# First weights behind two input tiles, own tiles for the third and fourth job's weights, and a measuring stream ahead of the split

## The chip, the cores and the metric

The kernel runs on one core of one Trainium2 chip, in one launch. The metric is the device time of an execution in microseconds (us). Engine names: TensorE is PE (its weight loads are PEld), VectorE is DVE, ScalarE is ACT, GpSimd is POOL, and SyncE is SP, whose queue issues the transfers.

## The reference

One layer of a streaming encoder trunk over 2048 prompt frames and 32 sample frames, D = 1024. What matters here is its start:

```python
hp = layer_norm(x_prompt, ln0_g, ln0_b)
qa, ka, va, za, qkv_b, zb, a_b, b_b, gate_a, gate_b = split_projection(x @ w_in)
```

The input is normalised and multiplied by `w_in`, of 1024 x 6160. Of the products, `gate_a` and `gate_b` (2 x 1024 columns) are needed only at the end; `a_b` and `b_b` (16 columns) give the decays of a gated delta rule (branch B), `qkv_b` its queries, keys and values through a causal convolution; the rest feeds chunk-band attention (branch A). Both branches are projected, gated, merged, projected again and normalised.

## The kernel before

Precision comes from splitting: each float32 operand becomes a half-precision high part and a half-precision rest, and a product is three passes on TensorE (high by high, high by weights' rest, input's rest by high). Weights are first scaled by a power of two that comes from their own sum of squares.

The prompt is done in two halves of 1024 columns. `build_h` loads eight input tiles of 128 frames (512 KB each), takes mean and variance on VectorE, normalises there, transposes on TensorE, adds gain and bias on ScalarE (`q` = 0) or VectorE (`q` = 1) into `tmp`, casts to the high part `hi` on ScalarE and subtracts the rest `lo` on GpSimd. Tiles 4 to 7 take their statistics only after the mark `first`: the last `tmp` of tile 3 is written (line 534). The marks `h_ready` and `l_ready` say when a tile's parts are there.

A job is one tile of 128 weight columns (1024 x 128, in two transfers of 256 KB). `all_jobs` gives their order: in the first half two gate jobs, then `ab` (the 16 decay columns; its rest shares the tile `whi` with its high part, and it has two blocks of 512 columns), then the convolution's jobs. Three coroutines serve them:

- `fetch` loads `wraw` (two buffers, `raw_gate`),
- `divide` waits for a `whi`/`wlo` pair (two buffers, `w_gate`), and, in the first half, squares the weights on ScalarE with an accumulated sum `w_sq`; `power` sums over the partitions with a small matmul and makes the scale on VectorE, GpSimd (a power) and VectorE again; then ScalarE scales and casts and GpSimd subtracts, in two pieces of 512,
- `multiply` runs the passes, block by block; with the last block of a job it gives `w_gate` back. The first two jobs run together, in blocks of 256, 256 and 512 columns (`FIRST[0]`), each block for both jobs in turn. Results go to two banks (`pj`); a job's `evac` reads them and frees the bank.

The order of the instructions on each engine is fixed when the program is built, by a planner (`Flow`): every coroutine has a clock, each operation is priced, and the one with the earliest clock goes on. On the chip each engine runs its list in this order and waits for real semaphores. The planner prices a transfer on SyncE's queue so:

```python
start = max(self.cur.clock + 0.2, self.busy.get(queue, 0.0)) + 0.5
end = max(start + 0.6, self.busy.get("DMA", 0.0)) + size / 200e3
return end + MARGIN        # 1.6
```

where rows of under 768 bytes count as 768. `yield` with a number moves a coroutine's clock to that time. `flow.start(x, 2.0)` starts one at clock 2.0.

When `l_ready[0][7]` is set (the last `lo` of the first half), the main thread goes on: `phase_b` clears 17 block-diagonal tiles of 128 x 1024 on VectorE in one go (`k_bd`, `qk_bd`, `q_bd`, `kd_bd`, `u_bd`), and then opens the phase; only then can the `ab` job's `evac` run, which needs a tile of that phase (`open_job` waits for it). The phase's queue of blocks follows: decays, convolution, the delta rule's systems, its recurrence.

The profile puts nearly all instructions on line 260, a helper; so groups are told by their tiles: `whi` written from `wraw` with 128x1024 elements is the square, with 128x512 the cast; `wlo` the split; `b<-w_sq` the sum's matmul; `pj` the products; `sig` the gate jobs' evac; `ab` that of the decay columns.

Of the kernel before, what the change touches and what calls it, by code (L numbers as in the profile page):

```python
# [13 lines left out]
F16 = mybir.dt.float16  # L14
# [7 lines left out]
P = 128  # L22
D = 1024
KD = D // P
# [244 lines left out]
def trunk(ctx: ExitStack, tc: tile.TileContext, x_p, x_s, cache_k, cache_v, st_conv, st_gdn,  # L269
# [197 lines left out]
    def build_h(half, xpool, nx):  # L467

        hT[half] = [None, None]
        ncols = HCOLS[half]  # L470
        nt = 4 - half
        x_gate, t_gate = gate(nx), gate(nt)
        freed, first = [mark(), mark()], mark()
        sizes = [SPLIT, ncols - SPLIT]
        tiles = [(n + P - 1) // P for n in sizes]

        def free(b):
            yield h_free[b]
            w = SPLIT if b == 0 else HALF + DEC - SPLIT
            hT[half][b] = [hpool.tile([P, KD, w], F16, tag=f"{x}{b}", name=f"{x}{half}{b}") for x in ("hi", "lo")]  # L480
            freed[b].done()

        def one(b, t, rows):
            c0 = t * P
            gt = half * 8 + b * 4 + t
            xt = xpool.tile([P, D], F32, tag="x", bufs=nx, name=f"x{gt}")
            yield dma(xt[:rows], x_s if rows < P else x_p[gt * P:(gt + 1) * P, :])
            if half == 0 and b == 1:
                yield first
            st = xpool.tile([P, 2, 6], F32, tag="st", bufs=nx, name=f"st{gt}")  # L490
            for i in range(2):
                V.bn_stats(out=st[:rows, i, :], in_=xt[:rows, i * 512:(i + 1) * 512])
                yield
            V.bn_aggr(out=mv[:rows, gt, :], in_=st[:rows])
            V.tensor_scalar(out=mv[:rows, gt, 1:2], in0=mv[:rows, gt, 1:2], scalar1=LN_EPS,
                            scalar2=None, op0=ALU.add)
            yield
            rsqrt(mv[:rows, gt, 1:2], mv[:rows, gt, 1:2])
            yield
            V.tensor_scalar(out=xt[:rows], in0=xt[:rows], scalar1=mv[:rows, gt, 0:1],  # L500
                            scalar2=mv[:rows, gt, 1:2], op0=ALU.subtract, op1=ALU.mult)
            yield freed[b]
            hi, lo = hT[half][b]
            todo = [2, 2, 2]

            def part(q):
                tag = "ba"[q] if half == 0 else "b"
                yield t_gate
                yield scaled
                yield bank[tag]  # L510
                tp = pt(tag)
                for k in range(4):
                    kk = 4 * q + k
                    PE.transpose(tp[:, k * P:k * P + rows], xt[:rows, kk * P:(kk + 1) * P],
                                 ident[:rows, :rows])
                todo[0] -= 1
                if not todo[0]:
                    x_gate.give()
                yield
                tmp = xpool.tile([P, 4, P], F32, tag="tmp", bufs=nt, name=f"tmp{gt}{q}")  # L520
                m = tmp[:, :, 0:rows]
                ks = slice(4 * q, 4 * q + 4)
                for k in range(4):
                    kk = 4 * q + k
                    src, g, b_ = tp[:, k * P:k * P + rows], ln0gT[:, kk:kk + 1], ln0bT[:, kk:kk + 1]
                    if q == 0:
                        S.activation(out=tmp[:, k, 0:rows], in_=src, func=AF.Identity, scale=g, bias=b_)
                    else:
                        V.tensor_scalar(out=tmp[:, k, 0:rows], in0=src, scalar1=g, scalar2=b_,
                                        op0=ALU.mult, op1=ALU.add)  # L530
                    if k == 1:
                        yield
                bank[tag].give()
                if b == 0 and t == 3 and q == 1:
                    first.done()
                yield
                hv_ = hi[:, ks, c0:c0 + rows]
                S.copy(out=hv_, in_=m)
                todo[1] -= 1
                if not todo[1]:  # L540
                    h_ready[half][gt - half * 8].done()
                yield
                (V if q == 0 and half == 1 else G).tensor_tensor(out=lo[:, ks, c0:c0 + rows], in0=m,
                                                                 in1=hv_, op=ALU.subtract)
                t_gate.give()
                yield
                todo[2] -= 1
                if not todo[2]:
                    l_ready[half][gt - half * 8].done()

            for q in range(2):
                flow.start(part(q))

        for b in range(2):
            flow.start(free(b))
        for b in range(2):
            if half == 0 and b == 1:

                yield 3.0
            for t in range(tiles[b]):  # L560
                yield x_gate
                flow.start(one(b, t, min(P, sizes[b] - t * P)))

# [7 lines left out]
    class Job:  # L571
# [3 lines left out]
        def __init__(self, half, wid, src, evac=None, key=None, cols=P, blocks=None):  # L575
            self.wid = wid
            self.half, self.src, self.evac, self.cols, self.key = half, src, evac, cols, key
            self.end = self.two = False
            self.blocks = blocks or BLOCKS[half]

    NRAW = 2
    raw_gate, w_gate, sig_slots = gate(NRAW), gate(2), gate(2)
    q_raw, q_w = Queue(flow), Queue(flow)

    def fetch(jobs):

# [33 lines left out]
        V.tensor_scalar(out=inv, in0=half_, scalar1=h_scale[:, 2:3], scalar2=None, op0=ALU.mult)  # L620
        V.tensor_scalar(out=half_, in0=half_, scalar1=h_scale[:, 3:4], scalar2=None, op0=ALU.mult)

    def divide():

        while True:
            job, raw, t = yield from q_raw.get()
            yield w_gate
            hi = wpool.tile([P, KD, P], F16, tag="whi", bufs=2, name="whi")
            lo = wpool.tile([P, KD, P], F16, tag="wlo", bufs=2, name="wlo")
            sc = w_scale[:, job.wid:job.wid + 1]  # L630
            yield t
            if job.half == 0:
                S.activation(out=hi[:], in_=raw[:], func=AF.Square, accum_out=w_sq[:])
                yield
                yield from power(sc, w_sq[:])
                flow.start(factors(job.wid))
            src, main = raw[:, :, 0:job.cols], hi[:, :, 0:job.cols]
            S.activation(out=src, in_=src, func=AF.Copy, scale=sc)
            for i in range(2):
                ks = slice(4 * i, 4 * i + 4)  # L640
                S.copy(out=main[:, ks], in_=src[:, ks])
                yield

                rest_ = lo[:, ks] if job.cols == P else hi[:, ks, job.cols:P]
                G.tensor_tensor(out=rest_, in0=src[:, ks], in1=main[:, ks], op=ALU.subtract)
                if i:
                    raw_gate.give()
                    q_w.put((job, hi, lo))
                yield
# [14 lines left out]
    def multiply():  # L664

        while True:
            some, todo = [], [(0, 0)]
            while todo:
                bi, which = todo.pop(0)
                if which == len(some):  # L670
                    some.append((yield from q_w.get()))
                    job = some[which][0]
                    if which == 0:

                        todo = [(b, w) for b in range(len(job.blocks)) for w in range(1 + job.two)][1:]
                    if job.key:
                        job.open = mark()
                        flow.start(open_job(job))
# [16 lines left out]
                for k in range(KD):  # L695
                    PE.matmul(ps[:, 0:n], wh[:, k], hl[:, k, :], start=False, stop=(k == KD - 1))
                    if k == KD - 1:
                        last = bi == len(job.blocks) - 1
                        if job.end and (bi == 0 or last):
                            h_free[0 if bi == 0 else 1].give()  # L700
                        if last:
                            w_gate.give()
                    yield
                flow.start(evac(job, bi, c0, n, gcol, ps))
# [1234 lines left out]
    def marked():  # L1939

        ahead, half = [], None
        for job in all_jobs():
            if job.half != half:
# [3 lines left out]
                ahead, half, n = [], job.half, 0  # L1947
                job.two = True
            n += 1
            if n <= 2:  # L1950
                if job.key is None:
                    job.blocks = FIRST[half]
# [262 lines left out]
            all_done.done()  # L2215


    with ExitStack() as stack0:
        open_banks(stack0, "ps0", a=3)
        xp = stack0.enter_context(tc.tile_pool(name="x0", bufs=1, reuse_waits="tile"))  # L2220
        flow.start(norm_params(xp))
        flow.start(build_h(0, xp, 8))
        flow.start(fetch(marked()), 2.0)
        flow.start(setup(xp), 20.0)
        flow.start(setup2(xp), 30.0)
        flow.start(spread(), 100.0)
        flow.start(divide())
        flow.start(multiply())
        flow.run(l_ready[0][7])
    for half in range(2):  # L2230
        stack, make, done = phase_b(half)
        enter(1, half, make)
        flow.run(done)
        stack.close()
        if half:
            wr_pool.append(ctx.enter_context(tc.tile_pool(name="wr0", bufs=1)))
            wr_open.done()
# [70 lines left out]
```

## Time and profile before

| | before |
|---|---|
| median of 3 runs | 2084.61 us (2081.7 to 2089.64) |
| profiled execution, its own time | 2083.65 us |
| its span | 2081.6 us |
| TensorE busy | 1968.6 us (95%) |
| VectorE busy | 1499.7 us (72%) |
| ScalarE busy | 978.1 us (47%) |
| GpSimd busy | 633.1 us (30%) |
| moved by DMA | 196.49 MB, mean 94 GB/s |

The share of busy time is a mean over stages. TensorE is busy nearly all the time, so time can be found only where it idles; a row of the timeline gives the start in us, the duration, the engine, what is written from what, and, in brackets, the idle time before it and what ended that.

### The profile page before, as it was taken

How to read it: one execution, taken by the hardware profiler on the slowest of the kernel's cores; microseconds unless marked ns; L12 is line 12 of the kernel's file. 1: busy time of each engine (PE TensorE's matmuls, PEld its weight loads, DVE VectorE, ACT ScalarE, POOL GpSimd, SP SyncE). 2: the span in 40 equal slices, each digit the busy share in tenths (PEclk: the TensorE clock that was granted, in tenths of full speed). 3: DMA queues.
4: the chain of work that ended last, by engine and by line, in shares of the span. 5: the costliest groups of instructions: out<-in, count | busy, mean ns of one | idle time of the engine just before them, and what ended most of it. 6: DMA issues, size and time to landing. Idle time of an engine off the chain costs nothing. (4 is left out here: it accounts for less than half of the span.)

```text
span 2081.6 us, 41386 instructions
## 1 busy us (share of the span) xinstructions
PE 1968.6 (95%) x15098; PEld 1411.3 (68%) x15098; DVE 1499.7 (72%) x4661; ACT 978.1 (47%) x2098; POOL 633.1 (30%) x708
## 2 busy tenths in 40 slices
PE   4999999999999999998999999999999988999998
PEld 3454666766465657566667777667666777888996
DVE  7679889873377758679998986356656667666775
ACT  5565554444466667564544543355656641111110
POOL 6244333422312113243332331311011134433342
PEclk9999999999999999999999999999999999999999
DMA  3233232323423233122233233332232445433331
GB/s 119 72 92 106 75 102 57 100 80 91 116 86 111 70 92 100 65 85 72 66 89 83 77 99 84 105 92 76 72 88 88 129 137 175 132 102 122 102 116 54
DMA packets 197719, 196.49 MB, mean 94 GB/s; under 512 B 79622, under 2 KB 147570, under 8 KB 197516
## 3 DMA queue, kind: packets, MB, share of 16 engines
q1 hardware_dynamic: 197516, 193.85, 31.6%
q8 instruction: 119, 1.95, 0.4%
q14 instruction: 84, 0.69, 0.1%
HBM read 135.91 MB, written 50.53 MB: 90 GB/s over the span
## 5 line engine op out<-in xcount | busy, mean ns | idle before, releaser
L260 PE MATMUL pj<-hi,whi 128*128 128x512 f16 (+2 forms) x1992 | 644.8, 339 | 10.4 <-DVE zb L260 2.7
L260 PE MATMUL pj<-hi,wlo 128*128 128x512 f16 (+2 forms) x1952 | 635.9, 338 | 2.4 <-POOL wlo L260 2.3
L260 PEld LDWEIGHTS <-whi 128*128 128x128 f16 x3984 | 413.5, 105 | 214.5 <-issue 3.9
L260 PE MATMUL pj<-lo,whi 128*128 128x512 f16 (+2 forms) x1992 | 457.7, 340 | 0.0
L260 POOL TENSOR_TENSOR wlo<-wraw,whi 128x512 f16<-128x512 f32 x192 | 226.9, 1184 | 585.9 <-ACT whi L260 313.0
L260 PEld LDWEIGHTS <-wlo 128*128 128x128 f16 x1952 | 204.8, 105 | 111.1 <-issue 10.7
L260 ACT CAST mh<-sg 128x256 fp32r<-128x256 f32 x64 | 25.9, 406 | 279.6 <-DVE sg L260 279.6
L260 ACT CAST ph<-b 128x512 f16<-128x512 f32 (+2 forms) x224 | 93.1, 421 | 100.0 <-PE b L260 96.8
L260 DVE TENSOR_TENSOR pl<-b,ph 128x512 f16<-128x512 f32 (+2 forms) x224 | 107.7, 485 | 44.7 <-ACT ph L260 43.1
L260 PE MATMUL a<-ghi,whi 128*128 128x256 f32 (+1 forms) x512 | 132.6, 290 | 6.3 <-DVE sg L260 6.2
L260 DVE TENSOR_TENSOR sys_u<-sys_u,sys_t 128x60 f32<-128x60 f32 (+23 forms) x527 | 129.3, 251 | 6.7
L260 ACT ACTIVATE wraw<-wraw,w_scale 128x1024 f32<-128x1024 f32 (+1 forms) x98 | 111.5, 1138 | 46.6 <-DVE w_scale L260 42.9
L260 PE MATMUL a<-ghi,wlo 128*128 128x256 f32 (+1 forms) x512 | 130.3, 285 | 0.0
L260 ACT CAST whi<-wraw 128x512 f16<-128x512 f32 (+1 forms) x196 | 119.4, 612 | 20.9 <-PE pj L260 18.0
L260 DVE TENSOR_TENSOR sys_t<-sys_u,sys_p 128x60 f32<-128x60 f32 (+21 forms) x459 | 121.2, 265 | 6.1
L260 ACT ACTIVATE sb<-sb,mx,unit 128x640 f32<-128x640 f32 (+4 forms) x128 | 108.8, 851 | 20.0 <-DVE mx L260 19.7
L260 DVE SCALAR_TENSOR_TENSOR acc<-raw,cwT,acc 128x512 f32<-128x512 f32 x144 | 114.0, 792 | 5.4 <-ACT acc L260 4.4
L260 POOL TENSOR_TENSOR w_scale<-w_scale,mhalf 128x1 f32<-128x1 f32 x49 | 30.9, 631 | 269.3 <-DVE w_scale L260 204.2
L260 PE MATMUL b<-ident,sb 128*128 128x128 f32 x560 | 100.6, 279 | 5.3 <-ACT sb L260 2.2
L260 PEld LDWEIGHTS a<-ghi,whi 128*128 128x128 f32 x512 | 98.0, 191 | 9.0 <-DVE sg L260 7.8
L260 ACT COPY v_t<-o 128x64 f32<-128x64 f32 x132 | 27.7, 210 | 161.1 <-PE o L260 133.3
L260 PEld LDWEIGHTS a<-ghi,wlo 128*128 128x128 f32 x512 | 97.8, 191 | 0.3
(350 smaller groups left out, 4221.8 us busy)
## 6 DMA issues: line engine op xcount, KB each, us to landing
wraw<-in_w_in SPq DMA_DIRECT2D x192, 256.0 KB
sg<-sig SPq DMA_DIRECT2D x112, 128.0 KB
sig<-sig SPq DMA_DIRECT2D x44, 256.0 KB
sys_p<-sol_p SPq DMA_DIRECT2D x17, 512.0 KB
x<-in_x_p SPq DMA_DIRECT2D x16, 512.0 KB
xt<-in_x_p SPq DMA_DIRECT2D x16, 512.0 KB
out_y_p<-xt SPq DMA_DIRECT2D x16, 512.0 KB
glo<-g SPq DMA_DIRECT2D x14, 512.0 KB
```

The lines of the kernel that those rows point to most:

```text
L260: r = f(*a, **k)
```

## The change

- `fetch` starts at the planner's clock 1.0 instead of 2.0, and `build_h` issues the first half's tiles 2 and 3 only at 2.0. So the transfers of the first two jobs' weights stand behind input tiles 0 and 1, ahead of 2 and 3; tiles 4 to 7 follow as before.
- The third job (`ab`) and the fourth get tiles of their own from a new pool `first_w` (6 KB per partition), which is opened ahead of the first stage's pool and closed after branch B's first half. They neither wait for `w_gate` nor give it.
- `divide` is cut in two: `measure` takes a job from `fetch`, waits for its tiles and its data, squares and makes the scale; `divide` takes it from there by a queue `q_scaled`. Behind a square the planner's clock is moved on by 0.4.
- The first two jobs' run takes in the third: the order of (block, job) is (0,0), (1,0), (0,1), (1,1), (0,2), (2,0), (2,1), (1,2), where it was (0,0), (0,1), (1,0), (1,1), (2,0), (2,1).

```diff
@@ build_h
             for t in range(tiles[b]):
+                if half == 0 and b == 0 and t == 2:
+                    yield 2.0
                 yield x_gate
                 flow.start(one(b, t, min(P, sizes[b] - t * P)))
...
-    q_raw, q_w = Queue(flow), Queue(flow)
+    q_raw, q_scaled, q_w = Queue(flow), Queue(flow), Queue(flow)
...
-    def divide():
+    def measure():
 
         while True:
             job, raw, t = yield from q_raw.get()
-            yield w_gate
-            hi = wpool.tile([P, KD, P], F16, tag="whi", bufs=2, name="whi")
-            lo = wpool.tile([P, KD, P], F16, tag="wlo", bufs=2, name="wlo")
+            if job.own:
+                hi, lo = job.own
+            else:
+                yield w_gate
+                hi = wpool.tile([P, KD, P], F16, tag="whi", bufs=2, name="whi")
+                lo = wpool.tile([P, KD, P], F16, tag="wlo", bufs=2, name="wlo")
             sc = w_scale[:, job.wid:job.wid + 1]
             yield t
             if job.half == 0:
                 S.activation(out=hi[:], in_=raw[:], func=AF.Square, accum_out=w_sq[:])
-                yield
+                yield flow.cur.clock + 0.4
                 yield from power(sc, w_sq[:])
                 flow.start(factors(job.wid))
+            q_scaled.put((job, raw, hi, lo))
+            yield
+
+    def divide():
+
+        while True:
+            job, raw, hi, lo = yield from q_scaled.get()
+            sc = w_scale[:, job.wid:job.wid + 1]
             src, main = raw[:, :, 0:job.cols], hi[:, :, 0:job.cols]
...
                         todo = [(b, w) for b in range(len(job.blocks)) for w in range(1 + job.two)][1:]
+                        if job.blocks is FIRST[0]:
+
+                            todo = [(1, 0), (0, 1), (1, 1), (0, 2), (2, 0), (2, 1), (1, 2)]
...
-                        if last:
+                        if last and not job.own:
                             w_gate.give()
...
             n += 1
+            if half == 0 and 2 < n <= 4:
+                job.own = [first_w.tile([P, KD, P], F16, name=f"{x}{n}") if x == "whi" or job.cols == P else None
+                           for x in ("whi", "wlo")]
+            if half == 0 and n == 3:
+                yield job
+                continue
...
+    stack_w = ExitStack()
+    first_w = stack_w.enter_context(tc.tile_pool(name="first_w", bufs=1, reuse_waits="tile"))
...
-        flow.start(fetch(marked()), 2.0)
+        flow.start(fetch(marked()), 1.0)
...
+        flow.start(measure())
         flow.start(divide())
...
         stack.close()
+        stack_w.close()
```

More of the change, by code (lines that the diff above doesn't have):

```diff
@@ L578, in __init__ @@
             self.end = self.two = False
+            self.own = None
             self.blocks = blocks or BLOCKS[half]
```

## The prediction

> **What bounds the kernel now.** I read the page first: its head, then the line of TensorE in part 1 and in the 40 slices.
>
> ```profile
> span 2081.6 us, 41386 instructions
> ...
> PE 1968.6 (95%) x15098; PEld 1411.3 (68%) x15098; DVE 1499.7 (72%) x4661; ACT 978.1 (47%) x2098; POOL 633.1 (30%) x708
> ...
> PE   4999999999999999998999999999999988999998
> ```
>
> TensorE is busy 1968.6 of 2081.6 us and has a 4 in one slice alone, the first. So the kernel is bound by TensorE, and a change of the start can win only what TensorE idles there. The busy times by stretch (columns: stretch, its length, each engine's busy time, granted clock) say how much that is.
>
> ```profile
> 0.00:20.00 20.00, 5.59 (x23) 4.68 (x24) 14.56 (x51) 7.71 (x15) 7.83 (x15) 1.00 0.73 272
> 20.00:40.00 20.00, 11.42 (x67) 9.23 (x65) 17.81 (x50) 13.72 (x31) 15.05 (x16) 1.00 0.08 10
> 40.00:60.00 20.00, 15.56 (x95) 11.14 (x96) 15.42 (x27) 9.31 (x20) 9.41 (x8) 0.83 0.15 48
> 60.00:80.00 20.00, 16.67 (x80) 7.51 (x79) 9.76 (x20) 10.74 (x18) 6.60 (x9) 1.00 0.23 76
> 80.00:100.00 20.00, 19.90 (x148) 9.77 (x146) 13.81 (x33) 17.43 (x25) 5.68 (x10) 1.00 0.18 64
> ```
>
> Of the first 80 us TensorE idles 80 - 5.59 - 11.42 - 15.56 - 16.67 = 30.8 us; from 80 us on it is full (19.90 of 20). From 0 to 40 VectorE is the busy one (17.81 of 20 in the second stretch): it normalises eight input tiles. Now the timeline of TensorE, at the places where the blocks of the first jobs begin.
>
> ```profile
> 31.64 0.42 PE L260 MATMUL pj<-hi,whi 128*128 128x256 f16 x1
> ...
> 48.35 0.33 PE L260 MATMUL pj<-hi,wlo 128*128 128x256 f16 x1 [1.94 <-POOL wlo L260]
> ...
> 49.75 1.92 PE L260 MATMUL pj<-lo,whi 128*128 128x256 f16 x8
> ...
> 53.41 1.04 PE L260 MATMUL pj<-lo,whi 128*128 128x256 f16 x8
> ...
> 56.91 0.38 PE L260 MATMUL pj<-hi,whi 128*128 128x512 f16 x1
> ...
> 62.09 0.38 PE L260 MATMUL pj<-hi,whi 128*128 128x512 f16 x1
> ...
> 70.45 1.47 PE L260 MATMUL pj<-hi,whi 128*128 128x512 f16 x6 [2.67 <-POOL whi L260]
> ...
> 74.06 1.89 PE L260 MATMUL pj<-hi,whi 128*128 128x512 f16 x8
> ...
> 77.51 0.38 PE L260 MATMUL pj<-hi,whi 128*128 128x512 f16 x1
> ...
> 79.62 0.38 PE L260 MATMUL b<-w_sq,tiny 128*128 128x1 f32 x2 [0.65 <-ACT whi L260]
> ```
>
> The first weights serve from 31.64, the second only from 48.35 (1.94 us of wait for their low half), the blocks of the second half of the columns run at 56.91 and 62.09, the third job (the 16 decay columns) waits 2.67 us for its weights and takes 70.45 to 77.51, and the fourth job begins at 77.51. That last time is my yardstick: whatever stands behind it is a full TensorE.
>
> Why the weights are late is in the timelines of ScalarE, GpSimd and VectorE.
>
> ```profile
> 17.66 1.05 ACT L260 ACTIVATE whi<-wraw 128x1024 f16<-128x1024 f32 x1
> 24.48 1.15 ACT L260 ACTIVATE wraw<-wraw,w_scale 128x1024 f32<-128x1024 f32 x1 [0.45 <-DVE w_scale L260]
> 25.66 0.62 ACT L260 CAST whi<-wraw 128x512 f16<-128x512 f32 x1
> 34.34 1.05 ACT L260 ACTIVATE whi<-wraw 128x1024 f16<-128x1024 f32 x1
> 62.29 1.06 ACT L260 ACTIVATE whi<-wraw 128x1024 f16<-128x1024 f32 x1 [4.66 <-PE pj L260]
> 67.87 0.69 ACT L260 ACTIVATE sig<-pj,w_half 128x512 f32<-128x512 f32 x1 [3.85 <-issue]
> ```
>
> ```profile
> 42.69 1.16 POOL L260 TENSOR_TENSOR wlo<-wraw,whi 128x512 f16<-128x512 f32 x1
> ...
> 48.26 2.27 POOL L260 TENSOR_TENSOR lo<-tmp,hi 128x512 f16<-128x512 f32 x2
> ```
>
> ```profile
> 24.56 0.68 DVE L260 BATCH_NORM_STATS2 st<-x 128x6 f32<-128x512 f32 x1
> ...
> 44.99 1.37 DVE L260 TENSOR_SCALAR tmp<-a,ln0gT,ln0bT 128x128 f32<-128x128 f32 x4 [2.44 <-POOL lo L260]
> 46.52 0.91 DVE L260 MEMSET k_bd<- 128x1024 f32 x1 [0.16 <-issue]
> ...
> 63.71 0.91 DVE L260 MEMSET u_bd<- 128x1024 f32 x1 [0.16 <-issue]
> ...
> 65.30 0.15 DVE L260 TENSOR_SCALAR w_scale<-w_scale 128x1 int32<-128x1 int32 x1 [0.67 <-POOL w_scale L260]
> 75.68 0.74 DVE L260 SCALAR_TENSOR_TENSOR ab<-pj,w_inv,ab 40x512 f32<-40x512 f32 x1 [1.94 <-ACT ab L260]
> ```
>
> The squares that measure jobs 1, 2 and 3 stand at 17.66, 34.34 and 62.29; the third had to wait until TensorE was through with the first weights (their tile is reused). The last low half of the input ends at 48.26 + 2.27 = 50.53. And right behind the last tile VectorE clears 17 block-diagonal tiles, 46.52 to 64.62 (63.71 + 0.91), in one piece: nothing that stands behind them in its order runs earlier.
>
> **The change part by part.**
>
> Order of the loads. Two rows of SyncE's queue, the second the third job's raw weights:
>
> ```profile
> 3.33 2.03 SPq L283 DMA_DIRECT2D wraw<-in_w_in  x4
> ...
> 35.99 2.03 SPq L283 DMA_DIRECT2D wraw<-in_w_ab  x4
> ```
>
> Four issues of 0.5 us go ahead of input tiles 2 and 3, and their 1 MB is about 3.9 us at the 272 GB/s of the first 20 us: tiles 2 and 3 land up to 4 us later. VectorE covers it with tiles 0 and 1 while it has work on them; without that cover it is the loss that stands below. The planner prices an input tile at 2.62 us, a weight tile at 2 x 1.97 (its 512-byte rows count as 768), one after another, plus 1.6. In its clock the first two weight tiles come at 13.7 and 17.6 instead of 18.9 and 22.9, input tiles 2 and 3 at 20.2 and 22.9 instead of 12.4 and 15.0, and tiles 4 to 7 as before. This clock sets only the order of the instructions. By it the first square moves among the work on tile 0, and the first split ends, by my own pass through the order, near 25 instead of 34; the second near 31 instead of 48. On the chip I take the same shifts. TensorE then has the first four 256-column blocks (2.6 us each, half of the 62.09 - 56.91 = 5.2 of a 512-column block; 10.4 in all) done among the transposes before tile 7 is ready. These blocks stop counting.
>
> Tiles 4 to 7 wait for the last of tile 3 (mark "first"). In the order their statistics move back from 25.5 to about 30.9. Real cost: VectorE loses the head start that it had on tiles 2 and 3 (two tiles, four statistics of 0.68 = 2.7 us), and ScalarE and GpSimd get back what the second job's scale, two casts and two splits took among tiles 4 to 7: 1.15 + 2 x 0.62 and 2 x 1.16, 2.4 us each. I take 49.5 for the last low half, 1 us earlier than the 50.53 of now; ends 47.5 (the 2.4 are won, nothing lost) and 53 (the 2.7 lost, nothing won).
>
> Third job. Its own tile takes away the wait at 62.29, and block 0 of it stands before the second half of the columns. In the order its raw weights land at 43.6 and its scale is through VectorE at about 47.5 to 48; the 17 clears are issued when tile 7 is done, at about 51.5 by the same pass. So the scale stands before the clears, by some 4 us of planner clock. Its split ends at about the same time as tile 7, so TensorE idles some us ahead of it.
>
> The sum, from 49.5 on, on TensorE alone. Start of the third job's block 0 at +0.5 (hand-over); the block 74.06 - 70.45 = 3.6, and 1.7 more for a slow start (below); block 2 of job 1: 62.09 - 56.91 = 5.2; the same of job 2: 5.2; block 1 of job 3: 77.51 - 74.06 = 3.45. There are two result banks. Block 0 of job 3 keeps one until its reader runs, and that reader is behind the clears on VectorE; so the next three blocks share one bank, and each of two hand-overs costs the reader's 0.69 (row at 67.87) and about 0.3 on both sides, 1.0. Sum: 0.5 + 5.3 + 5.2 + 1.0 + 5.2 + 1.0 + 3.45 = 21.7, so the fourth job begins at 71.2: 6.3 us before 77.51.
>
> What could be late next: the bank, free after the clears and one reading of 0.74, 64.62 + 0.74 = 65.4, before 71.2. And the fourth job's weights: in the order the second half of their measuring falls at about 51 to 52.5, on the clears' edge. Behind them the chain is 64.62 + 0.15 + 1.15 + 0.62 + 1.16 = 67.7 with about 1 us of hand-overs, 68.7: covered by 71.2, but by 2.5 us only; 3 us on the clears would cost 0.5. Their own tiles and job 3's leave the fifth job's weights earlier too, which no row shows as a wait today: 0.
>
> The clock of TensorE: eight matmuls of 256 columns took 1.92 us at 49.75, soon after the wait of 1.94, and 1.04 us at 53.41; after the 2.67 us wait six of 512 took 1.47 at 70.45, which is the fast pace. The slow pace lasted from 48.35 to 49.75 + 1.92 = 51.67, so a slow start costs about half of 3.3 us, 1.7. I charge one, ahead of job 3, and none for the hand-overs of 1.0. [...]
>
> The split of measuring from scaling, and the 0.4 us that the planner now allows behind each square: the power matmul is placed later and finds its sum ready. The waits of TensorE from 80 to 200 us show the price of now.
>
> ```profile
> PE b L260 <- ACT whi L260: 3.2, 4, 1.5
> ```
>
> Four waits; 0.4 off each is 1.6 at most and 0 at least, and the 0.65 at 79.62 goes with the early measuring. I take 1.7 for both. VectorE, ScalarE and GpSimd do the same instructions as before; the new stream is one of the planner and adds no instruction.
>
> Total: 6.3 + 1.7 = 8.0 us, ends 0 + 77.51 - 74.7 = 2.8 (last low half at 53) and 77.51 - 65.5 + 2.3 = 14.3 (at 47.5, no slow start, no bank hand-over). The profiled execution took 2083.65 us (span 2081.6), 1 us under the median 2084.61; from the profile 2075.7, from the median 2076.6.
>
> **The rivals.**
>
> A. Slower: the third job's scale lands behind the clears. The place is VectorE's order at tile 7; it decides when GpSimd's power for the third job ends, in the planner's clock, after tile 7 does. For it: GpSimd is full there (15.05 of 20 from 20 to 40) and the margin is 4 us of a pass by hand. Against it: extra work on GpSimd delays tile 7 as well. Price: scale at 64.8, 0.7 + 0.4 + 2 x 0.67 for scaling, casting and splitting narrow halves (estimate: half of the rows above) and 1 of hand-overs, 68.2; TensorE then still has 3.6 + 1.7 + 5.2 + 5.2 + 3.45 = 19.2 before the fourth job, at 87.4: 10 us later than now. 2084.6 + 10 - 1.6 = 2093.
>
> B. The gain is given back. The front is won, but later stages wait for something that does not move with it, and the order of everything behind the start is planned anew. For it, over the whole trace:
>
> ```profile
> PE x L260 <- DVE r L260: 14.5, 17, 2.3
> ```
>
> the recurrence waits for VectorE 17 times; against it: it begins with the third and fourth job's results, which come earlier too. Half to all of 8 us lost, 2080 to 2085; I put it at 2083.
>
> C. The whole front is won: tile 7 early, no slow start, and hand-overs covered: 14.3 us, 2070.3.
>
> **How the numbers follow.** My forecast 0.45 (2076.6, its own range 2072 to 2081), A 0.13, B 0.22, C 0.20. Half a per cent is 10.4 us: below 2074.2 is faster, about what a measurement of this kernel can tell. C and a third of the forecast are below that: 0.35. Above 2095 are half of A and a little of B: 0.09. Same: 0.56. The range goes from 2067, some us under C for the new order behind the start, to 2091, which leaves most of A out.
>
> **What would show it.** Right: the first square near 12 to 14, first pj matmul near 22 to 26, the third job's block before 56, the 17 clears between, two waits of about 1 us of TensorE for ScalarE's sig, and the fourth job at 70 to 73. Wrong: w_scale of the third job behind the last clear and a TensorE gap of over 10 us ahead of the third job (A); the fourth job at 71 and a span that does not follow, with more wait for r, state and vn (B); the last low half later than 53 (the head start on tiles 2 and 3 was worth more than I took).

## The result and the profile after

The changed kernel takes 2103.19 us (median of 6 runs, 2094.52 to 2109.4), beside 2085.48 us for the kernel before (6 runs, 2081.7 to 2089.64): a ratio of 1.0083, interval 1.0059 to 1.0108. It is slower by 0.8%, clear of the spread. The forecast of 2076.6 us had the wrong sign, and the time is outside its range of 2067 to 2091. The profiled execution took 2104.26 us (span 2102.4), 20.6 us above that of before.

The head of the page, and TensorE's line of it:

```profile
span 2102.4 us, 41380 instructions
...
PE 1979.9 (94%) x15098; PEld 1420.8 (68%) x15098; DVE 1498.9 (71%) x4661; ACT 977.3 (46%) x2098; POOL 636.7 (30%) x708
```

The work is the same: 15098 matmuls, the other engines within 4 us. The span grew by 20.8 us: TensorE is busy 1979.9 - 1968.6 = 11.3 us longer with the same matmuls, and idles 9.5 us more; its mean granted clock is 0.977 where it was 0.988. So half of the loss is waiting and half is matmuls at a lower clock. But for 1.7 us of a slow start, the prediction looked for time only where TensorE idles; the second half is outside that.

Busy times of the first 100 us by stretch, columns as before:

```profile
0.00:20.00 20.00, 4.97 (x21) 4.35 (x21) 11.24 (x47) 9.66 (x18) 7.43 (x15) 1.00 0.73 272
20.00:40.00 20.00, 15.02 (x90) 11.34 (x91) 16.34 (x45) 9.49 (x22) 15.10 (x16) 0.83 0.19 44
40.00:60.00 20.00, 12.33 (x75) 8.03 (x73) 14.65 (x32) 14.02 (x33) 12.38 (x13) 0.79 0.13 41
60.00:80.00 20.00, 16.20 (x70) 6.84 (x68) 13.07 (x20) 4.21 (x6) 0.00 (x0) 0.96 0.07 27
80.00:100.00 20.00, 18.46 (x107) 8.73 (x108) 10.49 (x29) 16.32 (x24) 8.23 (x12) 0.91 0.24 75
```

From 20 to 40 us TensorE now does 15.02 instead of 11.42. The granted clock of that row is 0.83 where it was 1.00, but the 1.00 is not to be read as full speed: a matmul of 256 columns took 0.42 us at 31.64 before, as it does at 21.22 now, and 0.27 where the pace is fast. From 60 to 80 GpSimd does nothing at all and ScalarE 4.21; both wait. VectorE does 13.07 there, mostly the 17 clears, which run from 53.92 to 72.01. TensorE's timeline:

```profile
21.05 0.37 PE L260 MATMUL pj<-hi,whi 128*128 128x256 f16 x1
...
52.98 0.58 PE L260 MATMUL b<-w_sq,tiny 128*128 128x1 f32 x2 [4.95 <-ACT whi L260]
53.42 1.87 PE L260 MATMUL pj<-hi,whi 128*128 128x512 f16 x4
56.98 1.89 PE L260 MATMUL pj<-hi,whi 128*128 128x512 f16 x4 [1.69 <-POOL whi L260]
58.66 3.40 PE L260 MATMUL pj<-lo,whi 128*128 128x512 f16 x8
61.90 0.38 PE L260 MATMUL pj<-hi,whi 128*128 128x512 f16 x1
...
68.02 0.38 PE L260 MATMUL pj<-hi,whi 128*128 128x512 f16 x1 [0.78 <-ACT sig L260]
...
74.14 1.89 PE L260 MATMUL pj<-hi,whi 128*128 128x512 f16 x8 [0.78 <-ACT sig L260]
...
81.40 0.38 PE L260 MATMUL b<-w_sq,tiny 128*128 128x1 f32 x2 [3.65 <-ACT whi L260]
81.64 0.38 PE L260 MATMUL pj<-hi,whi 128*128 128x512 f16 x1
...
82.80 0.63 PE L260 MATMUL pj<-hi,whi 128*128 128x512 f16 x1
...
88.37 1.13 PE L260 MATMUL b<-ident,ab 40*64 40x40 f32 x32
```

The first weights serve from 21.05 (before: 31.64). The third job begins at 53.42, at the slow pace (eight low passes of 512 columns in 3.40 us), and the two blocks behind it change banks with waits of 0.78. Then TensorE stands for 3.65 us, and the fourth job begins at 81.64 instead of 77.51. VectorE and ScalarE show why:

```profile
48.96 0.14 DVE L260 TENSOR_SCALAR w_scale<-w_scale 128x1 int32<-128x1 int32 x1
...
53.60 0.16 DVE L260 TENSOR_SCALAR w_scale<-b 128x1 f32<-128x1 f32 x1 [3.30 <-PE b L260]
53.92 0.91 DVE L260 MEMSET k_bd<- 128x1024 f32 x1 [0.16 <-issue]
...
71.10 0.91 DVE L260 MEMSET u_bd<- 128x1024 f32 x1 [0.16 <-issue]
71.93 0.10 DVE L260 TENSOR_SCALAR w_scale<-w_scale 128x1 int32<-128x1 int32 x1
```

```profile
12.22 1.06 ACT L260 ACTIVATE whi<-wraw 128x1024 f16<-128x1024 f32 x1
...
50.70 0.74 ACT L260 ACTIVATE wraw<-wraw,w_scale 128x512 f32<-128x512 f32 x1
51.47 0.40 ACT L260 CAST whi<-wraw 128x256 f16<-128x256 f32 x1
51.78 1.05 ACT L260 ACTIVATE whi<-wraw 128x1024 f16<-128x1024 f32 x1
...
52.83 1.12 ACT L260 CAST hi<-tmp 128x512 f16<-128x512 f32 x2
...
77.79 0.68 ACT L260 ACTIVATE ab<-pj,w_inv 40x512 f32<-40x512 f32 x1 [2.99 <-PE pj L260]
78.50 1.15 ACT L260 ACTIVATE wraw<-wraw,w_scale 128x1024 f32<-128x1024 f32 x1
```

The third job's scale (48.96) stands before the clears. The fourth job's is cut in two by them: VectorE takes its sum at 53.60, having waited 3.30 us for it with the clears behind it, runs 17 clears, and finishes the scale at 71.93. That is not yet the wait of 3.65. The scale is there at 72.03, but ScalarE has the scaling behind the third job's second evac (77.79), for which it waits 2.99 us, so these weights are scaled only from 78.50; the wait ends with the fifth job's square, which follows the scaling and the first cast on ScalarE at 80.20. And the last high part of the input (52.83) stands behind the third job's scaling and cast and the fourth job's square; the last low half is

```profile
53.51 2.27 POOL L260 TENSOR_TENSOR lo<-tmp,hi 128x512 f16<-128x512 f32 x2 [0.83 <-ACT hi L260]
```

on GpSimd, done at 55.78 (before: 50.53).

But the start is the smaller part. The spans are cut here where 10, 30 and 60% of the 5936 products with `whi` or `wlo` (in `pj`) have begun; the busy times of these stages, before:

```profile
0.00:189.70 189.70, 154.22 (x880) 87.03 (x881) 148.06 (x395) 112.78 (x197) 82.75 (x106) 0.98 0.30 95
189.70:610.10 420.40, 405.05 (x2982) 262.50 (x2981) 306.22 (x1168) 209.97 (x428) 133.69 (x160) 0.99 0.32 87
610.10:1043.10 433.00, 415.58 (x3329) 273.96 (x3328) 327.99 (x1028) 266.14 (x547) 121.29 (x166) 0.99 0.29 85
```

After:

```profile
0.00:193.80 193.80, 157.53 (x879) 87.10 (x880) 146.36 (x399) 110.23 (x195) 82.44 (x105) 0.94 0.29 91
193.80:627.30 433.50, 411.13 (x2979) 270.70 (x2978) 305.55 (x1158) 210.24 (x430) 136.93 (x161) 0.96 0.31 86
627.30:1066.20 438.90, 419.45 (x3333) 276.69 (x3331) 331.23 (x1036) 267.05 (x548) 121.44 (x166) 0.98 0.28 83
```

The stages lose 4.1, 13.1 and 5.9 us: 23.1, of which the rest of the span gives 2.3 back. In the second stage, which begins 112 us behind the fourth job's first product, TensorE is busy 6.1 us longer and idles 22.4 instead of 15.4 us. Most of the new idle time is in waits of the delta rule's recurrence; TensorE's wait for `r` in this stage was, before,

```profile
PE x L260 <- DVE r L260: 5.6, 6, 2.3
```

and is, after,

```profile
PE x L260 <- DVE r L260: 11.8, 10, 3.6
```

### The profile page after: what moved, and what is told of

Same layout as the page of the kernel before. It is cut to its first block, busy times and chain, and to the rows that moved or that the text cites. A ratio compares the mean times of both kernels' runs of the same rounds, so it can differ in the third digit from the quotient of the medians.

```text
span 2102.4 us, 41380 instructions
## 1 busy us (share of the span) xinstructions
PE 1979.9 (94%) x15098; PEld 1420.8 (68%) x15098; DVE 1498.9 (71%) x4661; ACT 977.3 (46%) x2098; POOL 636.7 (30%) x708
## 3 DMA queue, kind: packets, MB, share of 16 engines
HBM read 135.91 MB, written 50.53 MB: 89 GB/s over the span
## 5 line engine op out<-in xcount | busy, mean ns | idle before, releaser
L260 PE MATMUL pj<-hi,whi 128*128 128x512 f16 (+2 forms) x1992 | 653.8, 343 | 13.5 <-ACT hi L260 4.7
L260 PE MATMUL pj<-hi,wlo 128*128 128x512 f16 (+2 forms) x1952 | 643.7, 342 | 0.4 <-POOL wlo L260 0.4
L260 DVE TENSOR_TENSOR sys_u<-sys_u,sys_t 128x60 f32<-128x60 f32 (+22 forms) x527 | 130.8, 254 | 6.5
L260 DVE CUSTOM_DVE_ANT_0 sb<-a,bias 128x320 f32<-128x320 f32 (+4 forms) x128 | 61.6, 486 | 54.4 <-PE a L260 54.0
```

The costliest lines, as they stand in the source:

```text
L260: r = f(*a, **k)
```

## The experiments

Two theories stood against each other. Theory S: the loss is made in the start, by the clears that cut the fourth job's scale and by what this delays. Theory P: the loss is made by the planner, which orders everything behind the start anew after any edit; the order of before happens to run well, and many others do not.

Ratios are against the kernel before, run on the same chip, with their intervals. Stages are of one profiled execution each, which lies within 7 us of its kernel's median, so a difference of a few us between stages is not read by itself.

**The three parts one by one**, on the kernel before. Load order alone:

```diff
+                if half == 0 and b == 0 and t == 2:
+                    yield 2.0
...
-        flow.start(fetch(marked()), 2.0)
+        flow.start(fetch(marked()), 1.0)
```

> The kernel before with the new order of the first loads alone. If the loss is made at the start by the fourth job's weights (theory S), this part is harmless: the third and fourth job still wait for the first two jobs' tiles, the first product begins some 8 us earlier, and the time is 2080 to 2088. If most of the loss comes from the order behind the start being planned anew (theory P), the time is not tied to the start and may be anything from 2075 to 2105, with the difference made after 200 us.

Measured 2091.36 us, 1.002 (1.0005 to 1.0036), 3 us above the 2080 to 2088 of theory S. The first weights come early, but the third job's still need a tile that is given back; in TensorE's timeline their sum's matmul is at 57.94, VectorE takes it behind the last clear at 67.32, and the block waits for the split:

```profile
70.34 2.74 PE L260 MATMUL pj<-hi,whi 128*128 128x512 f16 x6 [8.11 <-POOL whi L260]
```

The measuring stream and the 0.4 alone:

```diff
+    def measure():
...
                 S.activation(out=hi[:], in_=raw[:], func=AF.Square, accum_out=w_sq[:])
-                yield
+                yield flow.cur.clock + 0.4
...
+            q_scaled.put((job, raw, hi, lo))
```

> The kernel before with the measuring in a stream of its own and the 0.4 us behind each square. Theory S: within 4 us of before, since a job's tiles come free no earlier. Theory P: a start as before to within 1 us, and still a difference of more than 5 us, either way, made after 200 us.

Measured 2102.13 us, 1.0066 (1.0046 to 1.0087): nearly the whole loss of the change, by a kernel whose start gains, where theory P expected it unchanged. Its stages:

```profile
0.00:186.10 186.10, 152.34 (x859) 87.50 (x860) 142.50 (x362) 109.06 (x190) 80.46 (x103) 0.94 0.29 92
186.10:628.20 442.10, 418.10 (x2999) 270.52 (x2998) 319.82 (x1195) 210.81 (x433) 137.63 (x163) 0.95 0.30 86
```

It has 10% of the products 3.6 us earlier than the kernel before, and then takes 21.7 us longer for the next 20%. The waits there are others than the changed kernel's: 9.9 us for `v_t` instead of for `r`:

```profile
PE b L260 <- POOL v_t L260: 9.9, 4, 5.5
```

Own tiles and the block order alone:

```diff
+            if half == 0 and 2 < n <= 4:
+                job.own = [first_w.tile(...) ...]
...
+                            todo = [(1, 0), (0, 1), (1, 1), (0, 2), (2, 0), (2, 1), (1, 2)]
```

> The kernel before with the own tiles of the third and fourth job and the new order of blocks alone. Theory S: this is the part that puts the fourth job's scale behind the 17 clears of VectorE and the third job ahead of the second half of the columns; the fourth job begins at 81 or later instead of 77.5 and the time is 2095 to 2106. Theory P: the start loses the same 4 us, and the rest is open.

Measured 2100.08 us, 1.0055 (1.0037 to 1.0074). Here the loss is in the start. VectorE, then TensorE:

```profile
51.38 0.16 DVE L260 TENSOR_SCALAR w_scale<-b 128x1 f32<-128x1 f32 x1 [3.54 <-PE b L260]
...
69.72 0.10 DVE L260 TENSOR_SCALAR w_scale<-w_scale 128x1 int32<-128x1 int32 x1
```

```profile
71.93 2.74 PE L260 MATMUL pj<-hi,whi 128*128 128x512 f16 x6 [14.17 <-POOL whi L260]
```

Now it is the third job's scale that the clears cut in two, and TensorE waits 14.17 us for it. That is rival A of the prediction, in a kernel where the loads do not come early; 10% of the products have begun 13.2 us late.

**The clears one by one.** On the changed kernel, the 17 clears of the first half are issued from a stream of their own, one at a time, so that the planner can put other work between them; the phase opens without waiting for them, and the clears stand nowhere else:

```diff
-                V.memset(t[:], 0.0)
+                if half:
+                    V.memset(t[:], 0.0)
...
+                clear.append(t)
...
+        def clears():
+            for t in clear:
+                V.memset(t[:], 0.0)
+                yield
...
+        if half == 0:
+            flow.start(clears())
```

> The changed kernel, with the 17 clears of the first half issued one by one from a stream of their own, so that scales can stand between them, and the phase opens without waiting for them. The fourth job's scale is then ready near 57 and the third job's bank is freed at once: the fourth job begins at 75 to 77 instead of 81.6. Theory S: most of the loss goes, 2080 to 2090. Theory P: the start gains 5 to 6 us, and the total differs from 2103 by something else than that, by more than 5 us either way.

Measured 2078.04 us (2076.36 to 2084.8), 0.9962 (0.9943 to 0.9981): faster than both kernels, and 2 us below the 2080 to 2090 of theory S. VectorE has the fourth job's scale between the first two clears:

```profile
52.49 0.91 DVE L260 MEMSET k_bd<- 128x1024 f32 x1 [0.16 <-issue]
54.88 0.15 DVE L260 TENSOR_SCALAR w_scale<-w_scale 128x1 int32<-128x1 int32 x1 [1.48 <-POOL w_scale L260]
```

```profile
51.55 0.59 PE L260 MATMUL b<-w_sq,tiny 128*128 128x1 f32 x2 [4.95 <-ACT whi L260]
...
55.55 1.89 PE L260 MATMUL pj<-hi,whi 128*128 128x512 f16 x4 [1.68 <-POOL whi L260]
...
72.99 1.13 PE L260 MATMUL b<-ident,ab 40*64 40x40 f32 x32
```

On TensorE the waits of 4.95 and 1.68 ahead of the third job stay, the one of 3.65 ahead of the fourth is gone, and the decays' first transposes are at 72.99 instead of 88.37. The fourth job begins at 75.06, and 10% of the products have begun at 183.7 us: 10.1 us earlier than in the changed kernel, 6.0 earlier than before. So the place of the clears in the order makes the loss at the start, as theory S has it, and the start is worth up to 10 us. The edit does two things, though: the scale comes between the clears, and the phase opens early, so that the third job's bank is free at once; this run does not tell them apart. And 1.4 of the 10.1 us are there before any clear: the last low half ends at 54.35 instead of 55.78. Of the second stage it shows nothing by itself, since its order is a new one too. The same edit on the kernel before:

> The kernel before with the 17 clears issued one by one. It tells whether the changed kernel with such clears is fast by the clears alone. If the clears alone do it: 2075 to 2081 here as well. If the change and the clears need each other (the fourth job's scale stood behind them): the start is as before to within 2 us, and the time 2081 to 2090, apart from what theory P adds.

Measured 2083.02 us, 0.9989 (0.9973 to 1.0005): no change that can be told.

**The order alone.** The one edit is the planner's price of a load, which adds no work and removes none (15098, 4661, 2098 and 708 instructions on the engines, as before):

```diff
-MARGIN = 1.6
+MARGIN = 1.5     (plan_margin_15; 1.7 in plan_margin_17)
```

> The same control with 1.5. Theory P: more than 4 us away from before, by another amount than with 1.7; with the time made between 190 and 630 us and more slow clock of TensorE there. Theory S: within 4 us.

> A control: the kernel before, with the planner's allowance behind each transfer at 1.7 instead of 1.6. Nothing is added, moved between engines or made to wait; only the planner's clock differs, and so the order of instructions, mostly behind the start. Theory P (a new order by itself costs or gives several us in the delta rule's stage): more than 4 us away from before, either way, with a start within 2 us. Theory S (the start makes the loss): within 4 us.

Measured on the kernel before: 2112.68 us with 1.5 (1.0128, 1.0094 to 1.0163), 2098.73 with 1.7 (1.0059, 1.0043 to 1.0075). The stages with 1.5:

```profile
0.00:189.60 189.60, 154.25 (x879) 86.93 (x880) 148.31 (x396) 112.90 (x197) 82.30 (x106) 0.98 0.30 95
189.60:630.20 440.60, 415.13 (x2982) 267.46 (x2981) 312.64 (x1167) 209.24 (x427) 133.40 (x160) 0.96 0.30 83
...
1067.10:1693.50 626.40, 599.54 (x5326) 438.72 (x5324) 430.44 (x1565) 317.82 (x738) 143.74 (x154) 0.99 0.31 89
```

The start is equal to 0.1 us, and the next stage takes 20.2 us more, half of it idling and half matmuls of a lower clock (415.13 against 405.05 us), as in the changed kernel. An edit that changes nothing but the order can cost as much as this change did. That is theory P. With 1.7 the start is 0.7 us shorter and the second stage 7.2 us longer.

Not all of it is scatter. The stage from 60% to the last of these products takes 626.4 us with 1.5 and 624.7 with 1.7, where it took 615.6 before. It takes 624.7 to 626.4 in all five kernels with another price, changed or not, and 615.0 to 618.5 in all nine with 1.6: some 9 to 11 us there go with another price in whatever kernel, and the changed kernel has no part in them (617.1).

**The changed kernel in other orders.** Without the 0.4:

```diff
-                yield flow.cur.clock + 0.4
+                yield
```

> The changed kernel without the 0.4 us behind each square. Theory S: the start is the same to 1.5 us (fourth job at 80 to 83) and the time 2098 to 2106. Theory P: the same start, and a time more than 4 us away from 2103, since every power matmul of the first half stands elsewhere.

Measured 2085.19 us, 1.0001 (0.9982 to 1.002): 18 us come back with one number of the planner, where theory S expected none.

```profile
0.00:186.50 186.50, 151.92 (x864) 84.38 (x865) 139.31 (x367) 109.62 (x193) 79.53 (x106) 0.96 0.30 95
186.50:614.60 428.10, 410.69 (x2999) 268.56 (x2998) 315.05 (x1196) 212.65 (x432) 133.68 (x161) 0.97 0.31 87
```

In these stages 7.3 us of it are at the start (186.5 against 193.8) and 5.4 in the second (428.1 against 433.5): the 0.4 moves both, where both theories expected the same start. The start bears theory S out in another way: without the 0.4 the fourth job's scale stands ahead of the clears (53.89, the first clear at 54.90), its scaling is at 54.14, and the fourth job begins at 76.68, without the wait of 3.65, although the clears are in one piece and the phase opens behind them. With the other prices of a load:

> The same with 1.5: the same start; theory P again a total of its own. Of the two, against the kernel before with the same allowances (2099 and 2113), theory P has no fixed difference: it may change sign. A change that costs by itself is some 17 us above both, 2116 and 2130.

> The changed kernel with the planner's allowance behind a transfer at 1.7. If the 2103 of the changed kernel is mostly the order it happened to get behind the start (theory P), this one has the same start (fourth job near 81, 3 to 5 us late at 190 us) and another total, more than 4 us away from 2103, most likely below. If the change itself makes the rest slow, 2099 to 2107.

> The changed kernel with the clears issued one by one, at 1.7. Its start is the part that the change and the clears own: 5 to 7 us ahead of before at 190 us, as with 1.6. Theory P: the rest scatters, so the total is more than 4 us away from the 2078 with 1.6, most likely above. If the start carries through: 2076 to 2081.

| planner | kernel before | with the change |
|---|---|---|
| as it is (1.6) | 1 | 1.0083 (1.0059 to 1.0108) |
| price 1.7 | 1.0059 (1.0043 to 1.0075) | 1.0041 (1.0028 to 1.0055) |
| price 1.5 | 1.0128 (1.0094 to 1.0163) | 1.0085 (1.007 to 1.01) |
| clears one by one | 0.9989 (0.9973 to 1.0005) | 0.9962 (0.9943 to 0.9981) |
| clears one by one, 1.7 | not run | 0.9981 (0.9967 to 0.9995) |

In the first row the change costs 0.8%. In the other three it costs nothing that can be told: it comes out below its neighbour each time, with intervals that overlap. So the 17.7 us between the two kernels are no cost that the change carries with it; they belong to the one order that it was planned into, against the one of before. Three expectations missed here. With 1.7 the changed kernel's start was to be 3 to 5 us late and is 0.5 (190.2 against 189.7). With 1.5 theory P expected a total of its own, and 2103.55 us is the changed kernel's 2103.19 again; but it is made elsewhere, with a second stage 10.8 us shorter (422.7) and 9.3 us more in the stage from 60% on. And the clears one by one with 1.7 (2082.02 us) lie 4.0 us above those with 1.6, at the edge of what either theory gave.

**The same start, another order.** Own tiles for the third job only; the fourth takes the pair of the pool again:

```diff
-            if half == 0 and 2 < n <= 4:
+            if half == 0 and n == 3:
```

> The changed kernel with an own tile for the third job alone; the fourth waits for the first job's tile again. By theory S the fourth job's square no longer stands ahead of the third job's block on TensorE (the 5 us wait at 53 goes) and its scale comes behind the clears all the same: the third job's block begins 3 to 5 us earlier, the fourth job at 78 to 81. Theory P leaves the total open.

Measured 2083.68 us, 0.9986 (0.9972 to 1.0).

```profile
0.00:193.40 193.40, 157.78 (x888) 89.15 (x889) 146.88 (x401) 111.96 (x197) 82.72 (x107) 0.96 0.29 92
193.40:609.20 415.80, 402.61 (x2971) 263.13 (x2970) 302.45 (x1156) 208.28 (x426) 134.70 (x160) 0.98 0.32 90
```

TensorE ahead of the fourth job:

```profile
81.11 0.59 PE L260 MATMUL b<-w_sq,tiny 128*128 128x1 f32 x2 [3.65 <-ACT whi L260]
```

Its start is as late as the changed kernel's (193.4 against 193.8 us), but its second stage is 17.7 us shorter (415.8 against 433.5). Two kernels with the same late start are 20 us apart. This decides between the theories: S is true of the start, which explains 4 us of the loss, and P of the rest. Over all fourteen kernels the second stage takes 415.8 to 442.1 us; the kernel before, with 420.4, is the fourth shortest, the changed one, with 433.5, the third longest.

The start was expected to gain 3 to 5 us here, and did not. The wait ahead of the third job is 4.69 us, now for its split, and the wait of 3.65 ahead of the fourth is the same, although its scale is not cut: both halves stand behind the clears, done at 69.46, and the scaling at 78.21, again behind the third job's second evac. So the cut as such is not what costs; it is where ScalarE's order puts the scaling when the scale is planned behind the clears.

## Why the prediction was wrong

Three steps failed: the time of the last low half, the cover of the fourth job's weights, and the price put on a new order behind the start. Step by step:

- **First weights**: right in kind. The first square stands at 12.22 (forecast 12 to 14), the first product at 21.05 (22 to 26 was given; 1 us earlier), and the early 256-column blocks are done ahead of tile 7.
- **Last low half**: wrong, 55.78 us where 49.5 was put, with ends of 47.5 and 53. Tiles 4 to 7 were charged with the statistics' move alone. In the run these are at 29.71 instead of 24.56, and then ScalarE has 0.74 + 0.40 + 1.05 us of the third and fourth job's work (50.70 to 52.83) ahead of the last high part. The prediction credited the tiles with the work that leaves their stretch and did not debit the work of jobs 3 and 4 that comes into it. The order of the loads alone bears this out: it moves the statistics to 29.72 too, and the last low half ends at 43.07 + 9.19 = 52.26, inside the ends given.
- **Third job**: its scale stands before the clears (48.96), as forecast, so rival A did not happen. The block was to begin 0.5 us behind the input and take 5.3 us. It began at 53.42, ahead of the input's end, and took until 61.90, 8.5 us: the fourth job's sum stands ahead of it on TensorE (4.95 us of wait), it waits 1.69 for the second half of its own split, and nearly all its matmuls are slow. Moving the measuring forward put one more wait for ScalarE ahead of the third job; the prediction placed the measuring and did not ask what stands behind its matmul. Counted from the last low half, the early start and the long block cancel, by luck: the sum gives an end at 55.78 + 0.5 + 5.3 = 61.6.
- **Hand-overs of the bank**: right in kind, 0.78 us of wait each where 1.0 was charged; that no slow start was charged behind them was the author's estimate, and the granted clock was 1.00 there (61.71 to 82.19). So the sum holds from the last low half on: 55.78 + 21.7 = 77.5, and the third job's products end at 75.86 + 1.89 = 77.75. Two of its terms failed: its starting point, by 6.3 us, which is all that was to be won, and the cover of the fourth job's weights, by 4 us.
- **Fourth job's weights**: "covered by 2.5 us only" failed. The prediction saw that the measuring fell on the clears' edge, and priced the better side of it. The sum came before the clears and the end of the scale behind them, at 72.03. The split's chain of the prediction from there, 1.15 + 0.62 + 1.16 and 1 of hand-overs, would have ended at 76.0, ahead of 77.75; but ScalarE's order put the scaling behind one more evac (78.50), which the prediction did not look at. 3.65 us of wait and a slow stretch behind it follow. With the clears one by one this wait is gone, and the fourth job begins at 75.06, 2.5 us earlier than before and not 6.3; that 10% of the products have then begun 6.0 us earlier is near the forecast by luck.
- **The 0.4**: put at a gain of up to 1.6 us from four waits. Without it the changed kernel is 18 us faster (2085.19 against 2103.19), at the start too: as an edit of the plan it did much more than as a wait of 0.4.
- **Rival B** came true by half. The front was not won, as it says, but lost by 4.1 us; its other half, the order behind the start planned anew, made the rest of the loss, and its size was the error that cost most. It was held to "half to all of 8 us lost", 2080 to 2085, as if an order planned anew could only give back what the start had won. The two orders with another price of a load show +0.59 and +1.28%, 12 and 26 us, with nothing won or lost at the start; 7 and 20 us of it are made in the second stage, where the changed kernel lost 13.1. The 3.3 us by which the range went under C "for the new order behind the start" should have stood on both sides, and several times as large. Nothing in the trace of before could show this size, since it has one order; the sign of the result was not to be had from it.

Why one order idles more than another was followed only so far: the waits differ from kernel to kernel (`r` here, `v_t` with the measuring stream), and the three longest second stages (433.5, 440.6 and 442.1 us) have more idle time and a lower clock (0.95 to 0.96 against 0.99). Whether the lower clock comes from the gaps was not tried.

## What to carry to other kernels

Where a planner fixes the order of a whole kernel, an edit at the start is two edits: the one in the diff, and a new order behind it. Before crediting or blaming the first, measure the second: move a constant of the planner that has nothing to do with the change by a little in either direction, on both kernels, and take the spread (here 12 and 26 us up on the kernel before, 0 and about 9 us down on the changed one) as the least uncertainty of any forecast. Look at the stages of these controls too: the constant can have an effect of its own, as the 9 to 11 us here. Compare kernels stage by stage between anchors that are the same work in both, and keep long runs of off-path work, such as 17 clears, one each 1.07 us, out of one piece on an engine that the small steps of a critical chain share.

## What the runs showed of the hardware

TensorE's lower clock was a larger item than expected. In the row at 82.80 a matmul of 512 columns takes 0.63 us where 0.38 is usual; the granted clock is 0.50 from 82.19 to 85.61, shortly behind the wait of 3.65, which ended at 81.40. It is 0.50 from 51.47 to 61.71 too, and nearly all of the sixteen matmuls from 53.42 to 61.90, behind waits of 4.95 and 1.69, run at that pace. Over the span the same 15098 matmuls took 11.3 us longer than before. The slow stretch behind the 3.65 lasted 3.42 us, the one from 51.47 on 10.24 us, with the wait of 1.69 in it.

The waits alone do not sort these places. In the kernel before the granted clock fell to 0.50 at 48.46, for 3.41 us, with no wait over 1.94 in the 3.41 us ahead, and stayed at 1.00 through the wait of 2.67 that ended at 70.45. These are the prediction's two rows, the slow one behind 1.94 and the fast one behind 2.67. The busy time ahead does set them apart: TensorE was busy 0.72 us in the 3.41 us ahead of 48.46, and 0.79 us in as long ahead of the fall at 82.19 in the changed kernel, but 1.90 us from 68.93 to 72.35, where the clock stayed. In the changed kernel it was 0.50 from 54.88 to 58.30, with 1.73 us of busy time, and from 58.30 to 61.71, with TensorE busy all of the 3.41 us; from 61.71 on it was 1.00. These are five stretches of time in two traces; what makes the clock fall or come back was not shown.
